# Accumulating stores for the second halves of the attention heads, and accumulating DMAs for seven of nine additions in the last products

## Chip, cores and metric

The kernel runs on one core of one Trainium2 chip. Its engines are TensorE (PE in the profile; its weight loads are PEld), VectorE (DVE), ScalarE (ACT), GpSimd (POOL) and SyncE (SP); SP, ACT and POOL issue DMAs, each from its own queue and in order. The metric is the time of one execution on the device, in microseconds (us); less is better.

## The reference

One decoder layer over 1024 tokens of width 1024, in float32:

```python
xn = rms_norm(x)
proj = xn @ w_in                # q,k,v of 8 heads x 64 | q,k,v,gate,forget code of 4 gated heads | merge gates
o_sb = stick_breaking_attention(q, k, v)       # causal, 8 heads, out[t] = sum_s w[t,s] v[s]
o_gla = gated_linear_attention(...)            # chunks, state S_t = diag(a_t) S_{t-1} + k_t^T v_t
y = sigmoid(gate_sb + b0) * (o_sb @ w_branch_sb) + sigmoid(gate_gla + b1) * (o_gla @ w_branch_gla)
h = x + y @ w_out
u, g = split(rms_norm(h) @ w_ffn_in)
h = h + (gelu(causal_conv(u)) * g) @ w_ffn_out
out = rms_norm(h)
```

## The kernel before

A scheduling layer takes the kernel's Python statements, tracks which tile or stretch of DRAM each instruction reads and writes, sets an order for every engine and adds the waits. Each engine runs its own instructions strictly in that order; a DMA is issued when its queue's turn comes and its waits are over. Tiles come from pools of equal buffers: `t2` (128x512 float32, 11 buffers), `t4` (128x1024, 14), `t8` (128x2048, 16), `bank` (PSUM, 8). A new tile waits until all readers of the buffer's last tile are done, DMAs included.

All float32 products are made of three rounded ones: an operand is split in a high part and a rest (`split`: a cast on ACT, L122, and a subtraction on VectorE, L113), and `mac` (L205) or its kin multiply high by high, high by rest, rest by high. The large products use seven products of halves instead of eight, which costs sums and differences of tiles.

The stages touched:

*Attention* (345 to about 536 us). `attend` walks over 4 pairs of heads and 4 blocks of 256 tokens. `weigh` makes one chunk of scores: products (L828), a sigmoid on ACT (L830) into a `t2` tile, a scan on VectorE (L833, L835). Up to six chunks later `turn_weights` transposes them on TensorE (L842), and `gather` multiplies them by the values (L871). As the values are split in a high part and a rest side by side, the product `po` holds two halves of 64 partitions that must be added: the head's output is the sum. ACT takes `po` to a `t2` tile `o` (L877), and SP stores the two halves in two places of the DRAM tile `osb_d` (L879). `heads(th)` later loads both places for 512 tokens (L855), adds them (L119) and splits the sum: `heads(0)` runs beside the last heads, `heads(1)` in the next stage. Products of the gates (L205) fill TensorE between all these.

On POOL's queue run the loads of keys and queries (L737, `fetched`), of the gated branch (`gv_d`, `qd_d`, `ki_d`: L950, L952, L953), the first weights of the first branch (L181), and `kt_d` (L962).

*States of the gated branch* (from 538 us): `states` multiplies `kt` by values (L970); VectorE takes the result to the state (L977, L979), POOL scales it (L981).

*Last products* (1168 to 1378 us): 1024 x 2816 times 2816 x 1024, as seven products of halves in four phases, each over 11 blocks of the inner dimension (`phase`, L1343): `first`, `second`, `third`, `fourth`. The rows of the residual `h` lie in `hr`, loaded in the first phase. After a phase `first_done` or `second_done` copies two results per 128 tokens from PSUM to `c` and `d` on ACT and puts additions into `later`, which the next phase takes out two per block from its third block on. There are five additions after the first phase and four after the second for each of four groups of 128 tokens. The last two phases add their own results straight from PSUM, normalise and store.

Of the kernel before, what the change touches and what calls it, by code (L numbers as in the profile page):

```python
# [12 lines left out]
AF = mybir.ActivationFunctionType  # L13
ALU = mybir.AluOpType
# [3 lines left out]
P = 128  # L18
# [4 lines left out]
HALF = 512  # L23
# [45 lines left out]
def block_kernel(ctx: ExitStack, tc: tile.TileContext, x, norm_mix_g, w_in, b_gate, w_alpha_up, b_alpha,  # L69
                 gla_norm_g, w_branch_sb, w_branch_gla, w_out, norm_ffn_g, w_ffn_in, conv_w, conv_b,  # L70
                 w_ffn_out, norm_final_g, out):
    nc = tc.nc
    x, out = x[0], out[0]
# [6 lines left out]
    def nm(s):  # L80
        uid[0] += 1
        return f"{s}_{uid[0]}"
# [7 lines left out]
    def t8(dt=F32R):  # L90
        return sb.tile([P, 2 * D], dt, tag="t8", name=nm("t8"), bufs=16)

    def t4(dt=F32):
        return sb.tile([P, D], dt, tag="t4", name=nm("t4"), bufs=T4)

    def t2(dt=F32):
        return sb.tile([P, HALF], dt, tag="t2", name=nm("t2"), bufs=T2)

    def bank():
        return ps.tile([P, HALF], F32, tag="bank", name=nm("bank"), bufs=8)  # L100

    def dram(name, rows, cols, dt=F32):
        return dp.tile([rows, cols], dt, tag=name, name=name)

    def by(a, k):
        return a.rearrange("p (k c) -> p k c", k=k)

    def quarter():

        return [by(t8(), 4) for _ in range(2)]  # L110

    def sub(o, a, b):
        nc.vector.tensor_tensor(out=o, in0=a, in1=b, op=ALU.subtract)  # L113
# [4 lines left out]
    def add(o, a, b):  # L118
        nc.vector.tensor_tensor(out=o, in0=a, in1=b, op=ALU.add)  # L119

    def split(h, l, src):
        nc.scalar.copy(h, src)  # L122
        sub(l, src, h.bitcast(F32))
# [45 lines left out]
    osb_d = dram("osb_d", 2 * SBH * SBD, S)  # L169
# [388 lines left out]
    for half in range(2):  # L558
# [5 lines left out]
        o = t2()  # L564
# [162 lines left out]
    HALVES = slice(0, 64), slice(64, 128)  # L727
# [117 lines left out]
    ob, first_heads = [], []  # L845

    def heads(th):

        ob.append(quarter())
        asked, added = deque(), deque()  # L850
        for k in range(6):
            if k < 4:
                asked.append((t2(), t2()))
                for n, v in enumerate(asked[-1]):
                    nc.sync.dma_start(v, osb_d[n * HALF + k * P:n * HALF + (k + 1) * P, th * HALF:(th + 1) * HALF])  # L855
            yield
            if k > 1:
                split(*(a[:, k - 2] for a in ob[th]), added.popleft())
            if k in range(1, 5):
                a, b = asked.popleft()  # L860
                add(a, a, b)
                added.append(a)
            yield

    def gather(head, tp, ah, al):
        po = bank()
        nb = 2 * tp + 2
        for b in range(nb):
            c0 = 0 if b < nb - 1 else P
            for n, a in enumerate((ah, al)):  # L870
                nc.tensor.matmul(po[:, c0:2 * P], vt[b][:, head, :], a[b // 4][:, b % 4, c0:],  # L871
                                 start=(b == 0 and n == 0), stop=(b == nb - 1 and n == 1))
        o = t2()[:, 0:2 * P]
        for n in range(2):
            c = slice(n * P, (n + 1) * P)
            i = head * NT + 2 * tp + n
            nc.scalar.activation(o[:, c], po[:, c], AF.Identity, bias=vend[:, i:i + 1])  # L877
        for n, r in enumerate(HALVES):
            nc.sync.dma_start(osb_d[n * HALF + head * 64:n * HALF + (head + 1) * 64, tp * 2 * P:(tp + 1) * 2 * P], o[r])  # L879
        if head == SBH - 1 and tp == 1:  # L880
            first_heads.append(heads(0))

    def attend():
# [47 lines left out]
        while todo:  # L931
            flush()
            while late:
                gather(*late.popleft())
            for v in first_heads:
                next(v, None)
            yield 2
# [220 lines left out]
    n = 0  # L1158
    for _ in gated():
        if n == HEADS_AT:  # L1160
            fill(heads(1), 12)
        n += 1
        fill(first_branch, n % GLA[1] < GLA[0])
        pace(0)
# [119 lines left out]
    acts, hr = [], []  # L1284
# [44 lines left out]
    def row(i, j):  # L1329
        return hr[i][:, j * HALF:(j + 1) * HALF]  # L1330

    later, ready = deque(), deque()
# [33 lines left out]
    def temps(i):  # L1366
        return spare8[:, i], spare[i // 2][:, i % 2 * HALF:(i % 2 + 1) * HALF]

    def first_done(i, p1, p7):
        c, d = temps(i)  # L1370
        nc.scalar.copy(c, p1)
        nc.scalar.copy(d, p7)
        later.append(lambda: add(row(i, 0), row(i, 0), c))
        later.append(lambda: add(row(i, 1), row(i, 1), c))
        later.append(lambda: add(d, d, c))
        later.append(lambda: add(row(4 + i, 0), row(4 + i, 0), d))
        later.append(lambda: add(row(4 + i, 1), row(4 + i, 1), d))

    def second_done(i, p5, p6):
        c, d = temps(i)  # L1380
        nc.scalar.copy(c, p5)
        nc.scalar.copy(d, p6)
        later.append(lambda: add(row(4 + i, 0), row(4 + i, 0), d))
        later.append(lambda: add(c, c, d))
        later.append(lambda: add(row(i, 1), row(i, 1), c))
        later.append(lambda: add(row(4 + i, 1), row(4 + i, 1), c))

    gfin = []

# [25 lines left out]
            mul(row(4 + i, 1), row(4 + i, 1), gfin[0][:, HALF:])  # L1415

    def fourth_done(i, p4):
        r = row(4 + i, 0)
        sub(r, r, p4)
        o = spare[i % 2]  # L1420
        a, b = ss[i]
        nc.scalar.activation(o[:, :HALF], r, AF.Square, accum_out=b)
        add(a, a, b)
        nc.scalar.activation(b, a, AF.Sqrt, bias=eps, scale=1.0 / D)
        nc.vector.reciprocal(a, b)
        nc.scalar.activation(o[:, HALF:], row(4 + i, 1), AF.Copy, scale=a)
        nc.vector.scalar_tensor_tensor(out=o[:, :HALF], in0=r, scalar=a, in1=gfin[0][:, :HALF],
                                       op0=ALU.mult, op1=ALU.mult)
        t = slice((4 + i) * P, (5 + i) * P)
        if i < 3:  # L1430
            nc.gpsimd.dma_start(out[t, :], o)
        else:
            nc.sync.dma_start(out[t, :HALF], o[:, :HALF])
            nc.scalar.dma_start(out[t, HALF:], o[:, HALF:])

    for n, _ in enumerate(jobs):
        if n == 0:
# [9 lines left out]
    spare = [t4() for _ in range(2)]  # L1447
    spare8 = by(t8(F32), 4)
    phase(first, 2, 0, first_done, residual)
    phase(second, 2, 0, second_done, last_norm)  # L1450
    phase(third, 2, TILED[0], third_done)
    phase(fourth, 1, TILED[1], fourth_done, squares)


# [25 lines left out]
```

## Time and profile before

| | us |
|---|---|
| median of 3 runs | 1386.52 (1386.4 to 1386.62) |
| the profiled execution | 1386.67 |
| its span, first to last instruction | 1384.8 |
| TensorE busy | 1372.4 |
| VectorE busy | 1064.6 |
| ACT busy | 643.9 |
| POOL busy | 136.3 |

Views of the trace give times from the start of the span. A line of the list of waits names the waiting engine, the tile and line it waited in, and what ended the wait; then the sum in us, how many times, and the longest. A group has the number of its instructions, then busy us and the mean ns of one, then the idle time of the engine just before them. A timeline row has start, length, engine, line, operation, what is written and read, how many instructions it merges (xN), and in brackets the idle time before it. A DMA row ends in the size and the time from issue to landing. A row of a stretch has its limits, its length, then busy us and instructions of PE, PEld, DVE, ACT and POOL, then the granted clock of TensorE, the DMA engines' busy share and GB/s.

### The profile page before, as it was taken

Reading aid. Unit: us, or ns where it says so; the run is one execution under the profiler, and the core shown is the slowest. Engines: PE = TensorE matmul, PEld = TensorE weight load, DVE = VectorE, ACT = ScalarE, POOL = GpSimd, SP = SyncE. Lnnn points to the kernel's source line nnn. Section 1 sums busy time; section 2 is a strip of 40 time slices with the busy share of each in tenths; the row PEclk is TensorE's granted clock in tenths of the full one; section 3 lists DMA queues with packets and bytes.
Section 4 is the critical chain, followed back from the end, with each engine's and each line's share of the span. In section 5 each row is a group of like instructions: output and inputs, shape, how many; then the busy total and the mean of one; then the engine's idle time right before and its main releaser. Section 6 shows DMA issues by size and latency. Waiting matters only on the chain.

```text
span 1384.8 us, 18329 instructions
## 1 busy us (share of the span) xinstructions
PE 1372.4 (99%) x6559; PEld 1138.8 (82%) x6559; DVE 1064.6 (77%) x1640; ACT 643.9 (46%) x1244; POOL 136.3 (10%) x233
## 2 busy tenths in 40 slices
PE   9999999999999999999999999999999999999997
PEld 6788888888888888888888788888888888888886
DVE  6388688874878877658348998998888977896765
ACT  7334445653766664724126443343333334454654
POOL 2002123101111002200000000000000000000000
PEclk9999999999999999999999999999999999999999
DMA  6335278448776567673325245554444537953332
GB/s 239 132 117 151 84 221 251 143 158 210 216 158 151 131 197 237 198 237 136 136 91 177 52 120 187 196 189 152 150 163 152 182 107 272 322 163 102 99 101 105
DMA packets 164108, 227.92 MB, mean 165 GB/s; under 512 B 10938, under 2 KB 105276, under 8 KB 163506
## 3 DMA queue, kind: packets, MB, share of 16 engines
q1 hardware_dynamic: 134944, 139.01, 33.0%
q0 software_dynamic: 22496, 73.73, 16.8%
q10 hardware_dynamic: 6578, 14.03, 2.7%
q8 instruction: 51, 0.84, 0.3%
q14 instruction: 39, 0.32, 0.1%
HBM read 160.28 MB, written 66.45 MB: 164 GB/s over the span
## 4 chain that ended last, share of the span: by engine, by line
PE 95%; DVE 3%; ACT 1%; issue 0%; DMA 0%; ACTq 0%; DVEq 0%
PE bank L205 58%; PE bank L1343 15%; PE bank L385 6%; PE bank L1210 6%; PE bank L871 3%; PE bank L828 2%; PE bank L842 2%; DVE t L113 2%; PE bank L494 1%; PE bank L340 1%; DVE t L119 1%; PE bank L562 1%; PE bank L1007 1%; PE bank L970 0%; PE bank L994 0%
## 5 line engine op out<-in xcount | busy, mean ns | idle before, releaser
L205 PE MATMUL bank<-t,t 128*128 128x512 f32 x3624 | 861.1, 393 | 0.9 <-DVE t L113 0.7
L205 PEld LDWEIGHTS bank<-t,t 128*128 128x128 f32 x3624 | 676.5, 188 | 143.1 <-DVE t L113 1.6
L113 DVE TENSOR_TENSOR t<-t,t 128x512 fp32r<-128x512 f32 (+3 forms) x655 | 434.6, 697 | 93.5 <-ACT t L122 87.2
L122 ACT CAST t<-t 128x512 fp32r<-128x512 f32 (+1 forms) x543 | 320.3, 627 | 325.4 <-DVE t L113 81.0
L119 DVE TENSOR_TENSOR t<-bank,t 128x512 f32<-128x512 f32 x266 | 179.3, 685 | 97.9 <-PE bank L205 54.9
L1343 PE MATMUL bank<-t,t 128*128 128x512 f32 x924 | 209.6, 389 | 0.0
L1343 PEld LDWEIGHTS bank<-t,t 128*128 128x128 f32 x924 | 173.5, 188 | 36.0
L113 DVE TENSOR_TENSOR t<-bank,t 128x512 fp32r<-128x512 f32 (+4 forms) x124 | 69.5, 574 | 27.5 <-ACT t L122 26.9
L1210 PE MATMUL bank<-t,t 128*128 128x512 f32 x384 | 88.8, 391 | 0.0
L1241 ACT ACTIVATE t<-t,vcol 128x1024 f32<-128x1024 f32 x22 | 27.4, 1245 | 127.5 <-DVE t L119 127.5
L113 DVE TENSOR_TENSOR t<-t 128x512 f32<-128x512 f32 x120 | 83.3, 701 | 4.1 <-DMA t<-in_w_ffn_in_dram 3.7
L1210 PEld LDWEIGHTS bank<-t,t 128*128 128x128 f32 x384 | 71.6, 188 | 14.6
L119 DVE TENSOR_TENSOR t<-t,t 128x512 f32<-128x512 f32 x115 | 75.5, 686 | 9.8 <-ACT t L628 8.6
L122 ACT CAST t<-bank 128x512 fp32r<-128x512 f32 (+3 forms) x120 | 60.3, 512 | 48.8 <-PE bank L842 26.8
L385 PE MATMUL bank<-t,t 128*128 128x512 f32 x336 | 77.9, 391 | 0.0
L385 PEld LDWEIGHTS bank<-t,t 128*128 128x128 f32 x336 | 62.7, 188 | 13.1 <-DVE t L113 0.2
L1243 DVE SCALAR_TENSOR_TENSOR t<-t,vcol,t 128x1023 f32<-128x1023 f32 (+1 forms) x44 | 56.3, 1279 | 14.1 <-ACT t L1241 13.9
L833 DVE TENSOR_TENSOR_SCAN t<-t,t 128x128 f32<-128x128 f32 (+1 forms) x64 | 51.6, 816 | 17.5 <-ACT t L830 17.2
L828 PE MATMUL bank<-t,t 128*128 128x128 f32 (+3 forms) x192 | 54.6, 369 | 0.0
L842 PE MATMUL bank<-ident,t 128*128 128x128 f32 x288 | 53.2, 273 | 0.0
L871 PE MATMUL bank<-t,t 128*128 128x256 f32 (+1 forms) x320 | 51.0, 276 | 1.2 <-ACT t L122 0.7
L830 ACT ACTIVATE t<-bank 128x128 f32<-128x128 f32 (+3 forms) x96 | 46.9, 507 | 7.2 <-DMA osb_d<-t 3.2
(164 smaller groups left out, 813.5 us busy)
## 6 DMA issues: line engine op xcount, KB each, us to landing
t<-in_w_ffn_in_dram SPq DMA_DIRECT2D x50, 512.0 KB, 5.1
t<-in_w_in_dram SPq DMA_DIRECT2D x43, 512.0 KB, 5.3
act_d<-t POOLq DMA_DIRECT2D x22, 512.0 KB, 5.8
t<-in_w_ffn_out_dram SPq DMA_DIRECT2D x22, 512.0 KB, 7.6
wsum_d<-t POOLq DMA_DIRECT2D x22, 512.0 KB, 4.5
t<-act_d SPq DMA_DIRECT2D x22, 512.0 KB, 5.9
t<-wsum_d SPq DMA_DIRECT2D x44, 256.0 KB, 3.1
t<-in_w_ffn_out_dram SPq DMA_DIRECT2D x33, 256.0 KB, 2.7
```

The source lines that it names most:

```text
L113: nc.vector.tensor_tensor(out=o, in0=a, in1=b, op=ALU.subtract)
L119: nc.vector.tensor_tensor(out=o, in0=a, in1=b, op=ALU.add)
L122: nc.scalar.copy(h, src)
L205: nc.tensor.matmul(pt, a[:, kk], b[:, kk], start=start and kk == 0 and m == 0, stop=stop and kk == k - 1 and m == 2)
L385: nc.tensor.matmul(pt, a[:, k % 4, t], b, start=k == 0 and m == 0, stop=k == NK - 1 and m == 2)
L828: nc.tensor.matmul(z[:, 0:w], q[:, a, e, ts_], kk[:, e, b0 * P:b1 * P], start=a == 0, stop=a == 1)
L833: nc.vector.tensor_tensor_scan(out=kr, data0=kr, data1=above[:, 0:w], initial=1.0, op0=ALU.mult, op1=ALU.max)
L842: nc.tensor.transpose(pt[:, b * P:(b + 1) * P], ke[:, b * P:(b + 1) * P], ident)
L871: nc.tensor.matmul(po[:, c0:2 * P], vt[b][:, head, :], a[b // 4][:, b % 4, c0:], start=(b == 0 and n == 0), stop=(b == nb - 1 and n == 1))
L1210: nc.tensor.matmul(pt, a[:, k % 4, t], b, start=(k == 0 and m == 0), stop=(k == NK - 1 and m == 2))
L1243: nc.vector.scalar_tensor_tensor(out=cv[:, i:], in0=av[:, :S - i], scalar=col(V_CW, (2 - i) * NF + f), in1=cv[:, i:], op0=ALU.mult, op1=AL ...
L1343: nc.tensor.matmul(pts[m][i], a[:, t], b, start=(k == 0 and x_ == 0), stop=(k == NH - 1 and x_ == 2))
```

## The change

In `gather` the first half is stored to `osb_d` by SP as before, at the place of the sum, and the second half is stored by POOL to the same place with an addition done by the DMA. `heads` then loads one tile where it loaded two, and adds nothing. In the last products seven of the nine additions per 128 tokens become DMAs from POOL that add `c` or `d` to the rows in `hr`; the two that make a new `d` or `c` stay on VectorE. The last phase writes its output over `hr` instead of into `spare`.

```diff
     def heads(th):
-        asked, added = deque(), deque()
+        asked = deque()
         for k in range(6):
             if k < 4:
-                asked.append((t2(), t2()))
-                for n, v in enumerate(asked[-1]):
-                    nc.sync.dma_start(v, osb_d[n * HALF + k * P:n * HALF + (k + 1) * P, th * HALF:(th + 1) * HALF])
+                asked.append(t2())
+                nc.sync.dma_start(asked[-1], osb_d[k * P:(k + 1) * P, th * HALF:(th + 1) * HALF])
             yield
             if k > 1:
-                split(*(a[:, k - 2] for a in ob[th]), added.popleft())
-            if k in range(1, 5):
-                a, b = asked.popleft()
-                add(a, a, b)
-                added.append(a)
+                split(*(a[:, k - 2] for a in ob[th]), asked.popleft())
             yield
...
     def gather(head, tp, ah, al):
-        for n, r in enumerate(HALVES):
-            nc.sync.dma_start(osb_d[n * HALF + head * 64:n * HALF + (head + 1) * 64, tp * 2 * P:(tp + 1) * 2 * P], o[r])
+        dst = osb_d[head * 64:(head + 1) * 64, tp * 2 * P:(tp + 1) * 2 * P]
+        nc.sync.dma_start(dst, o[HALVES[0]])
+        nc.gpsimd.dma_start(dst, o[HALVES[1]], accum_op=ALU.add)
...
+    def onto(o, a):
+        nc.gpsimd.dma_start(o, a, accum_op=ALU.add)
+
     def first_done(i, p1, p7):
         c, d = temps(i)
         nc.scalar.copy(c, p1)
         nc.scalar.copy(d, p7)
-        later.append(lambda: add(row(i, 0), row(i, 0), c))
-        later.append(lambda: add(row(i, 1), row(i, 1), c))
+        onto(row(i, 0), c)
+        onto(row(i, 1), c)
         later.append(lambda: add(d, d, c))
-        later.append(lambda: add(row(4 + i, 0), row(4 + i, 0), d))
-        later.append(lambda: add(row(4 + i, 1), row(4 + i, 1), d))
+        later.append(lambda: onto(row(4 + i, 0), d))
+        later.append(lambda: onto(row(4 + i, 1), d))

     def second_done(i, p5, p6):
-        later.append(lambda: add(row(4 + i, 0), row(4 + i, 0), d))
+        onto(row(4 + i, 0), d)
         later.append(lambda: add(c, c, d))
-        later.append(lambda: add(row(i, 1), row(i, 1), c))
-        later.append(lambda: add(row(4 + i, 1), row(4 + i, 1), c))
+        later.append(lambda: onto(row(i, 1), c))
+        later.append(lambda: onto(row(4 + i, 1), c))
...
     def fourth_done(i, p4):
-        o = spare[i % 2]
-        nc.scalar.activation(o[:, :HALF], r, AF.Square, accum_out=b)
+        nc.scalar.activation(spare8[:, i], r, AF.Square, accum_out=b)
-        nc.scalar.activation(o[:, HALF:], row(4 + i, 1), AF.Copy, scale=a)
-        nc.vector.scalar_tensor_tensor(out=o[:, :HALF], in0=r, scalar=a, in1=gfin[0][:, :HALF], op0=..., op1=...)
+        nc.scalar.activation(q, q, AF.Copy, scale=a)
+        nc.vector.scalar_tensor_tensor(out=r, in0=r, scalar=a, in1=gfin[0][:, :HALF], op0=..., op1=...)
```

The lines behind `heads` move up by four or five: L877 becomes L872, L950 to L962 become L946 to L958, L970 becomes L966, L1343 becomes L1339. POOL's accumulating stores of the heads are L875, SP's plain ones L874, the last products' accumulations L1367.

The order in which the instructions stand on POOL, at the end of attention. `t4_1027` and `t4_1030` are first weights of the first branch, `t4_1035` and `t4_1037` the two halves of `kt`. Before:

```order
L953 DMA t8_964_4970<-ki_d_84 128x1024
L181 DMA t4_1027_5307<-in_w_branch_sb_dram 128x4x256
L181 DMA t4_1030_5315<-in_w_branch_sb_dram 128x4x256
L962 DMA t4_1035_5325<-kt_d_85 128x1024
L962 DMA t4_1037_5328<-kt_d_85 128x1024
L981 TENSOR_SCALAR t4_1036_5327<-t2_1033_5323,emid0_992 128x128
```

And now, with the outputs of the last five gathers (`t2_969` to `t2_1022`) between them; `kt` is now `t4_1031` and `t4_1033`:

```order
L875 DMA osb_d_88<-t2_969_4993 64x256
L875 DMA osb_d_88<-t2_992_5089 64x256
L181 DMA t4_1023_5295<-in_w_branch_sb_dram 128x4x256
L875 DMA osb_d_88<-t2_1014_5206 64x256
L875 DMA osb_d_88<-t2_1016_5228 64x256
L181 DMA t4_1026_5303<-in_w_branch_sb_dram 128x4x256
L875 DMA osb_d_88<-t2_1022_5282 64x256
L958 DMA t4_1031_5313<-kt_d_85 128x1024
L958 DMA t4_1033_5316<-kt_d_85 128x1024
L977 TENSOR_SCALAR t4_1032_5315<-t2_1029_5311,emid0_992 128x128
```

The two `kt` loads and the second weight load stand behind the accumulating stores of the last three gathers.

TensorE's order at the same place, with the semaphores that each row waits for, now:

```order
L205 MATMUL bank_1018_5242<-t8_59_336,t4_1003_5139 128x512
L966 MATMUL bank_1040_5338<-t8_963_4966,t4_1031_5313 128x256 [waits DMASW6_49,DMASW0_49]
L205 MATMUL bank_1043_5346<-t8_974_5015,t4_1024_5297 128x512 [waits PE_49,Activation_49]
L205 MATMUL bank_1043_5346<-t8_975_5016,t4_1024_5297 128x512
L205 MATMUL bank_1043_5346<-t8_974_5015,t4_1024_5297 128x512 [waits DVE_49]
L205 MATMUL bank_1043_5346<-t8_974_5015,t4_1024_5297 128x512
L205 MATMUL bank_1043_5346<-t8_975_5016,t4_1024_5297 128x512
L205 MATMUL bank_1043_5346<-t8_974_5015,t4_1024_5297 128x512
L966 MATMUL bank_1044_5353<-t8_963_4966,t4_1033_5316 128x256 [waits DMASW1_49,PE_49]
```

Before, the same nine stood there in the same order (as L205 and L970, with `t4_1035` and `t4_1037`): TensorE's order is kept, and the first reader of `kt` still stands thirteen matmuls of L205 behind the last gather.

The third place is ACT's order near the second head's output, with the waits. `t2_573` is the tile that a chunk's sigmoid (L830) writes. Before:

```order
L720 DMA gate_d_86<-t2_564_3213 128x512 [waits Activation_49]
L877 ACTIVATE t2_566_3225<-bank_565_3216,t2_478_2890 128x128
L830 ACTIVATE t2_570_3244<-bank_569_3241 128x256 [waits DMAHW7_49,DMAHW6_49]
L830 ACTIVATE t2_573_3255<-bank_572_3252 128x512 [waits DVE_49,PE_49]
L122 CAST t4_528_3081<-bank_582_3281 128x4x128 [waits PE_49]
```

And now:

```order
L720 DMA gate_d_86<-t2_564_3213 128x512 [waits Activation_49]
L872 ACTIVATE t2_566_3225<-bank_565_3216,t2_478_2890 128x128
L830 ACTIVATE t2_570_3244<-bank_569_3241 128x256 [waits DVE_49]
L830 ACTIVATE t2_573_3255<-bank_572_3252 128x512 [waits DMAHW5_49,DMASW5_49,PE_49]
L122 CAST t4_528_3081<-bank_582_3281 128x4x128 [waits PE_49]
```

The order is the same, but `t2_573` has got the buffer of the second head's output `t2_550`, and waits for its plain store (a DMA of SP's queue, HW) and its accumulating one (of POOL's, SW).

More of the change, by code (lines that the diff above doesn't have):

```diff
@@ L1417, in fourth_done @@
     def fourth_done(i, p4):
-        r = row(4 + i, 0)
+        r, q = row(4 + i, 0), row(4 + i, 1)
         sub(r, r, p4)
-        o = spare[i % 2]
         a, b = ss[i]
-        nc.scalar.activation(o[:, :HALF], r, AF.Square, accum_out=b)
+        nc.scalar.activation(spare8[:, i], r, AF.Square, accum_out=b)
         add(a, a, b)
@@ L1425, in fourth_done @@
         nc.vector.reciprocal(a, b)
-        nc.scalar.activation(o[:, HALF:], row(4 + i, 1), AF.Copy, scale=a)
-        nc.vector.scalar_tensor_tensor(out=o[:, :HALF], in0=r, scalar=a, in1=gfin[0][:, :HALF],
-                                       op0=ALU.mult, op1=ALU.mult)
+        nc.scalar.activation(q, q, AF.Copy, scale=a)
+        nc.vector.scalar_tensor_tensor(out=r, in0=r, scalar=a, in1=gfin[0][:, :HALF], op0=ALU.mult, op1=ALU.mult)
         t = slice((4 + i) * P, (5 + i) * P)
         if i < 3:
-            nc.gpsimd.dma_start(out[t, :], o)
+            nc.gpsimd.dma_start(out[t, :], hr[4 + i])
         else:
-            nc.sync.dma_start(out[t, :HALF], o[:, :HALF])
-            nc.scalar.dma_start(out[t, HALF:], o[:, HALF:])
+            nc.sync.dma_start(out[t, :HALF], r)
+            nc.scalar.dma_start(out[t, HALF:], q)
     for n, _ in enumerate(jobs):
```

## The prediction

> **What bounds the kernel now.** I read the page first: its span, the busy line, the granted clock and the chain that ended last.
>
> ```profile
> span 1384.8 us, 18329 instructions
> ...
> PE 1372.4 (99%) x6559; PEld 1138.8 (82%) x6559; DVE 1064.6 (77%) x1640; ACT 643.9 (46%) x1244; POOL 136.3 (10%) x233
> ...
> PEclk9999999999999999999999999999999999999999
> ...
> PE 95%; DVE 3%; ACT 1%; issue 0%; DMA 0%; ACTq 0%; DVEq 0%
> ```
>
> TensorE is busy for 1372.4 of 1384.8 us and makes up 95% of the chain. The second view is the list of TensorE's own waits, which says what there is to win:
>
> ```profile
> PE bank L464 <- DVE t L457: 1.6, 1, 1.6
> PE bank L435 <- POOL ident masks.py:199: 1.5, 1, 1.5
> PE bank L205 <- DVE t L113: 0.7, 1, 0.7
> PE bank L871 <- ACT t L122: 0.7, 1, 0.7
> PE bank L871 <- DVE t L113: 0.5, 1, 0.5
> ```
>
> TensorE waits 5.0 us in all. Two of the waits (L871, 0.7 and 0.5 us) lie where the diff works; the last-product phases (L1343) are not in the list. So work taken from VectorE is worth almost nothing, and a new wait on TensorE is paid in full, because its stream has no slack to give back. The question is what the change puts in front of TensorE.
>
> **Part 1: seven of nine additions in the last products.** VectorE loses 28 of 36 additions. Their price is in the groups of the second and third phases, and the matmuls' row of the page tells whether anybody waited:
>
> ```profile
> L119 DVE TENSOR_TENSOR t<-t,t 128x512 f32<-128x512 f32 x36 | 23.1, 684 | 0.3 <-ACT t L1382 0.3
> ```
>
> ```profile
> L1343 PE MATMUL bank<-t,t 128*128 128x512 f32 x924 | 209.6, 389 | 0.0
> ```
>
> They are the 36; 28 x 0.684 = 19 us of VectorE go, and TensorE idles 0.0 us before these 924 matmuls, so the gain is 0. What comes in its place is 28 accumulating DMAs of 256 KB on POOL's queue. The stretches in which they fall:
>
> ```profile
> 1228.00:1288.00 60.00, 60.00 (x266) 49.69 (x266) 45.75 (x75) 29.15 (x54) 0.00 (x0) 1.00 0.36 109
> 1288.00:1348.00 60.00, 60.00 (x267) 49.69 (x266) 42.71 (x69) 31.43 (x60) 1.07 (x2) 1.00 0.31 94
> ```
>
> POOL (0.00 and 1.07 us busy) and the DMA engines (share 0.36 and 0.31) are nearly free. 28 x 256 KB is 7.3 MB; even counted three times (read both, write one) it is 22 MB over 120 us, 183 GB/s beside the 109 and 94 moved now. The sums are read a phase later, up to 60 us after they start. Cover: the next phase's matmuls. I take 0; the bad end is a rival below. The last tile's output in place, instead of through `spare`, keeps the same instructions: 0.
>
> **Part 2: the heads' halves.** 32 of the 64 stores of `osb_d` (L879) move from SP to POOL and add to what SP's store has written; 8 of 16 reloads (L855) and 8 additions go. The additions go from ACT's and VectorE's path near the end of attention: ACT's splits there wait for them (ACT's waits between 520 and 545):
>
> ```profile
> ACT t L122 <- DVE t L119: 8.5, 2, 4.3
> ```
>
> ACT in order behind these splits feeds the 0.7 us of `L871 <- ACT t L122`. I take -0.7, with 0 and -1.2 (both L871 waits) as ends.
>
> Each accumulating store has to wait until its partner has landed, and POOL issues in order, so everything behind it on POOL stands. The order in the change's section shows what is behind the last three: one weight load of the first branch and both `kt_d` loads, which the state products (L970) read. Before, POOL's timeline there is:
>
> ```profile
> 526.20 0.77 POOL L181 DMA_DIRECT2D t<-in_w_branch_sb_dram  x1 [35.08 <-issue]
> 527.70 0.76 POOL L181 DMA_DIRECT2D t<-in_w_branch_sb_dram  x1 [0.72 <-PE bank L205]
> 528.82 1.17 POOL L962 DMA_DIRECT2D t<-kt_d  x2 [0.36 <-PE bank L871]
> ```
>
> And TensorE's, with the last head's gather at 533.44 and the first two users of `kt` at 538.20 and 540.02:
>
> ```profile
> 533.44 1.89 PE L871 MATMUL bank<-t,t 128*128 128x256 f32 x15
> 535.16 3.19 PE L205 MATMUL bank<-t,t 128*128 128x512 f32 x13
> 538.20 0.59 PE L970 MATMUL bank<-t,t 128*128 128x256 f32 x2
> 538.44 1.75 PE L205 MATMUL bank<-t,t 128*128 128x512 f32 x6
> 540.02 1.03 PE L970 MATMUL bank<-t,t 128*128 128x256 f32 x4
> ```
>
> The last gather leaves ACT, and SP stores it, here:
>
> ```profile
> 535.37 0.63 ACT L877 ACTIVATE t<-bank,t 128x128 f32<-128x128 f32 x2 [2.32 <-PE bank L871]
> ...
> 538.98 0.61 ACT L122 CAST t<-t 128x512 fp32r<-128x512 f32 x1
> ```
>
> ```profile
> 536.02 1.08 SPq L879 DMA_DIRECT2D osb_d<-t  x2
> ```
>
> The DMA view, asked for the moment of one issue, gives one landing: that store, the two `kt` loads, and the first branch's weights, a load of the same size on the same queue when it was emptier:
>
> ```profile
> osb_d<-t SPq DMA_DIRECT2D x1, 64.0 KB, 1.9
> ```
>
> ```profile
> t<-kt_d POOLq DMA_DIRECT2D x1, 512.0 KB, 5.5
> ```
>
> ```profile
> t<-kt_d POOLq DMA_DIRECT2D x1, 512.0 KB, 7.1
> ```
>
> ```profile
> t<-in_w_branch_sb_dram POOLq DMA_DIRECT2D x1, 512.0 KB, 3.9
> ```
>
> Now step by step. Store issued 536.0, landed 537.9. POOL issues the accumulating store, 0.6 us (half of 1.17 for two), and starts the first `kt` load at 538.5 instead of 528.8. It lands 5.5 later, at 544.0, and TensorE wants it at 538.2: 5.8 us of standing still, since the row behind L970 in TensorE's order can't pass it. The second load starts at 539.1 and lands 7.1 later, at 546.2; TensorE wants it 1.8 after the first: 545.8, another 0.4. Together 6.2 us. Ends: with 3.9 for both loads 542.4 - 538.2 = 4.2; with 7.1 for the first and 8.7 (the same 1.6 more) for the second, 7.4 + 0.4 = 7.8. I take 6.2, because SP's reloads of `osb_d` start in the same microseconds as they did around the loads of before. The second weight load has until 538.98, when ACT splits it: with 3.9 to land it may leave POOL as late as 535.1, 7.4 us later than before (527.70), so 0. The earlier shift of all this work doesn't help: the whole chain starts from TensorE's own gather.
>
> **The tiles held longer.** An output tile is freed when the accumulating store has landed, not the plain one. The tightest reuse I found is the second head's output: the next writer of its buffer is now a weigh sigmoid (L830), ACT's order shows its new wait. Rows: the store, issued behind the two loads of `x21_d`, the sigmoid pair, its scan, and TensorE's transposes of it:
>
> ```profile
> 363.06 1.09 SPq L879 DMA_DIRECT2D osb_d<-t  x2
> ```
>
> ```profile
> osb_d<-t SPq DMA_DIRECT2D x1, 64.0 KB, 7.4
> ```
>
> ```profile
> 371.29 0.86 ACT L830 ACTIVATE t<-bank 128x256 f32<-128x256 f32 x2
> ```
>
> ```profile
> 372.50 1.28 DVE L835 TENSOR_TENSOR_SCAN t<-t,t,zero 128x512 f32<-128x512 f32 x1
> ```
>
> ```profile
> 374.94 0.60 PE L842 MATMUL bank<-ident,t 128*128 128x128 f32 x4
> ```
>
> ```profile
> DMA to landing us min/median/max: 1.9/4.4/8.4
> ```
>
> The last row is of all 64 plain stores of L879. No row shows an accumulating store. It can't be quicker than a plain one of its size (1.9), since it reads its target too; the slowest, 8.4, is the other end; I take the median, 4.4. Store landed 370.5, accumulation landed 374.9, against the second sigmoid at 371.7 (half of the pair's time behind 371.29): ACT stands 3.2 us. TensorE has 374.94 - 373.78 = 1.2 us of slack behind the scan, so 2.0 reach it. Ends: 0 (with 1.9 ACT stands 0.7, inside the slack) and 6.0 (with 8.4).
>
> **The clock.** The granted clock in windows at the start and at the end:
>
> ```profile
> 4.90:8.30 3.40, 1.81 (x9) 0.83 (x9) 2.00 (x4) 2.55 (x6) 0.00 (x0) 1.00 1.04 404
> 8.30:11.70 3.40, 3.40 (x10) 2.00 (x9) 3.23 (x5) 3.37 (x8) 2.50 (x2) 0.50 1.05 401
> ...
> 1377.60:1380.40 2.80, 0.00 (x0) 0.00 (x0) 1.60 (x4) 1.61 (x4) 0.53 (x1) 1.00 0.47 187
> 1380.50:1384.80 4.30, 0.00 (x0) 0.00 (x0) 0.06 (x1) 0.03 (x1) 0.00 (x0) 0.50 0.33 122
> ```
>
> After 3.4 us with TensorE half idle the next 3.4 ran at 0.50, and at the end 0.50 was granted within 2.9 us of its last matmul. A stall of 6 us should bring one such stretch: at half speed 3.4 us lose 1.7. Part of it falls in the stall itself: I take 1.3, with 0 and 1.7 as ends. The Trainium skill (TensorE: Matmul & The Clock Gate, "What's actually happening") says that an idle window of about 3.4 us halves the clock until a busy one has passed; the two rows agree with it, and by the page alone the term would be 1.7, without the rule 0.
>
> **The sum.** +6.2 (kt) +2.0 (tile) +1.3 (clock) -0.7 (heads' additions) + 0 (last products) = +8.8. The profiled execution took 1386.67 us (span 1384.8 and 1.9 around it): 1395.5. It is 0.15 above the median of the runs, 1386.52, so the forecast is 1395.3. Ends: 4.2 + 0 + 0 - 1.2 = +3.0 gives 1389.5; 7.8 + 6.0 + 1.7 - 0 = +15.5 gives 1402.0.
>
> **Rivals.** *POOL isn't held* (not slower): if the accumulating stores were queued with their wait and POOL went on, the `kt` loads would start only three issues of 0.6 later, at 530.6 and 531.2, and land 5.5 and 7.1 behind that, at 536.1 and 538.3, before TensorE wants them at 538.2 and 540.0. The time would be 1386.5 - 0.7 = 1385.8. The point that decides: the first `kt` load has to leave POOL by 532.7 (538.2 - 5.5). Against it stands how POOL's loads of keys and queries behave now:
>
> ```profile
> L737 POOL DMA_DIRECT2D t<-sqkh_d x24 | 14.0, 588 | 116.6 <-PE bank L828 83.5 <-DVE t L113 29.3 <-PE bank L205 3.5
> ```
>
> POOL itself sat idle for 83.5 of 116.6 us until TensorE had let their buffers go. The Trainium skill (DMA: Bandwidth & Descriptors, "Anatomy of one DMA") says that the DMA engines don't wait on semaphores and the issuing sequencer does; by that rule this rival falls, and the row agrees. Chance 0.07.
>
> *Accumulating stores are slow* (8.4 us or more each): then the tile of the second head costs 6.0, and the same place recurs in later head pairs; counted twice more at half that, 6.0 more. 1395.3 + 4.0 + 6.0 = 1405.3. Nothing shows it, nothing excludes it. Chance 0.07.
>
> *The last products wait*: if the 256 KB accumulations went one after another at 8.4 us, the first phase's 16 would take 134 us where 60 are free, and the second phase's copies would stand 74 us: 1460. The free DMA share speaks against it. Chance 0.03.
>
> *A real gain* of over 2.8 us would have to come out of 1.9 us of TensorE's waits behind the start and the last tile's 7 us, which the change doesn't shorten. Chance 0.03.
>
> **How the numbers follow.** The forecast's case has 0.80 and lies wholly above 1389.3 (0.2%, 2.8 us, is about what a measurement of this kernel can tell from no change). The range is its bounds, 1389.5 to 1402.0, reached up to 1405.3 to take in the slow stores: it leaves out 0.13. Slower by over 0.2%: 0.80 + 0.07 + 0.03 = 0.90; within it 0.07; faster 0.03.
>
> **What would show it.** TensorE's waits should gain a line `L966 <- DMA t<-kt_d` of about 6 us near 540; POOL's timeline should show both `kt` issues behind the last accumulating store of L875; the granted clock should drop to 0.50 once behind that stall; ACT's L830 should wait some 3 us for `osb_d<-t` near 372; the four last phases should still run without TensorE idle. The prediction is wrong if `kt` leaves POOL before 533, or if a line of the last products (L1339) shows up among TensorE's waits.

## The result and the profile after

The changed kernel takes 1396.79 us (median of 4 runs, 1395.26 to 1396.95), the kernel before beside it 1386.56 us (1386.4 to 1386.62). The ratio is 1.0071, with a 95% interval of 1.0054 to 1.0089: slower, as forecast, and 1.5 us from the 1395.3 forecast. The profiled execution took 1396.89 us. Its page, the rows that answer to those shown of before:

```profile
span 1395.2 us, 18356 instructions
...
PE 1376.5 (99%) x6559; PEld 1140.7 (82%) x6559; DVE 1043.3 (75%) x1604; ACT 643.3 (46%) x1244; POOL 186.5 (13%) x293
...
PE 85%; DVE 6%; DMA 4%; issue 4%; ACT 1%; POOL 1%; SPq 0%; DVEq 0%; ACTq 0%; POOLq 0%
```

VectorE lost 21 us of work, and the span grew by 10.4. TensorE's share of the chain that ended last falls from 95% to 85%, and DMA, which had none, has 4%. TensorE's list of waits says where:

```profile
PE bank L966 <- DMA t<-kt_d: 7.7, 1, 7.7
...
PE bank L205 <- DVE t L113: 0.8, 1, 0.8
...
PE bank L1339 <- DVE t L113: 0.3, 1, 0.3
...
PE bank L842 <- DVE t L113: 0.3, 1, 0.3
```

One wait is new and large, for `kt`. The two waits at the gathers (L871, 0.7 and 0.5 us) have no counterpart of their size; two of 0.3 are new. POOL's timeline at the end of attention:

```profile
532.48 1.69 POOL L875 DMA_DIRECT2D osb_d<-t  x2 [6.73 <-ACT t L122]
533.74 1.26 POOL L181 DMA_DIRECT2D t<-in_w_branch_sb_dram  x1
538.93 0.83 POOL L875 DMA_DIRECT2D osb_d<-t  x1 [3.94 <-DMA osb_d<-t]
539.49 1.41 POOL L958 DMA_DIRECT2D t<-kt_d  x2
548.07 0.37 POOL L977 TENSOR_SCALAR t<-t,emid 128x128 f32<-128x128 f32 x1 [7.18 <-DVE t L973]
```

POOL stood for 3.94 us, released by `DMA osb_d<-t`: the landing of SP's plain store, the partner of the last accumulating one. Only then came the two loads of `kt`, at 539.5 and 540.1, where they had stood at 528.8 and 529.4. The landing of SP's store, asked for the moment of its issue, and that of the first `kt` load:

```profile
osb_d<-t SPq DMA_DIRECT2D x1, 64.0 KB, 2.4
```

```profile
t<-kt_d POOLq DMA_DIRECT2D x1, 512.0 KB, 6.5
```

TensorE resumes the moment it lands (539.49 + 6.5 = 546.0):

```profile
533.41 1.88 PE L866 MATMUL bank<-t,t 128*128 128x256 f32 x15
535.13 3.19 PE L205 MATMUL bank<-t,t 128*128 128x512 f32 x13
546.01 1.22 PE L966 MATMUL bank<-t,t 128*128 128x256 f32 x2 [7.68 <-DMA t<-kt_d]
546.67 3.12 PE L205 MATMUL bank<-t,t 128*128 128x512 f32 x6
```

The gather that starts it all ran at the same time as before (533.41 against 533.44): nothing earlier in the program had been lost by then. The last row shows a second loss. Six matmuls of L205 take 3.12 us where the same six took 1.75. The granted clock (the column ahead of the DMA share) in stretches of 3.4 us:

```profile
536.44:539.84 3.40, 1.88 (x9) 1.22 (x7) 0.26 (x1) 1.48 (x3) 0.91 (x2) 1.00 0.88 263
539.84:543.24 3.40, 0.00 (x0) 0.00 (x0) 1.04 (x2) 1.47 (x3) 1.05 (x2) 1.00 0.91 303
543.24:546.64 3.40, 0.63 (x2) 0.55 (x3) 0.00 (x0) 0.62 (x1) 0.00 (x0) 0.50 0.99 359
546.64:550.04 3.40, 3.40 (x10) 2.64 (x9) 0.58 (x2) 0.62 (x1) 0.37 (x1) 0.50 0.74 221
550.04:553.44 3.40, 3.40 (x17) 2.84 (x16) 1.96 (x6) 0.00 (x0) 0.74 (x2) 1.00 0.67 230
```

One stretch without a matmul, then two at half the clock: 10 matmuls in the fourth row, 17 in the fifth. The clock comes back 4.0 us after the matmuls did, which costs 2.0.

For the account, the start of each matmul was taken from both traces (6559 in each, nearly in the same order) and subtracted. The columns are the time in the kernel before at which the matmul starts, then the end of the last matmul and of the program; the rows are the delay in us, each set to 0 at 26.7 us, since the first 27 us differ by -0.4 to +0.35 from one execution to the next. The last column is the time from the end of the last matmul to the end of the program.

```
               377.0  460.5  532.8  538.2  544.7  555.1 1305.1 1311.9 |  last    end | tail
before          0      0      0      0      0      0      0      0    |  0      0    | 7.23
after           0.81   0.81  -0.37   7.48   9.47   9.46   9.37  10.38 | 10.38  10.04 | 6.89
e1_heads        1.82   1.82   0.23   7.89  10.36  10.36  10.36  10.36 | 10.36  12.62 | 9.49
e2_last        -0.02  -0.02  -0.02  -0.02  -0.02  -0.03  -0.03   0.79 |  0.79   1.42 | 7.86
e3_kt_ahead     0.82   0.82  -0.39  -0.40  -0.40   1.45   1.42   2.16 |  2.16   1.83 | 6.91
e4_pool_plain   0.00   0.00   0.01   5.09   7.83   7.83   7.82   7.82 |  7.82   9.98 | 9.39
e5_one_behind   0.37   0.37  -1.30   0.23   0.35   2.43   2.45   3.54 |  3.54   3.21 | 6.90
e6_plain_over   0.09   0.09  -1.59   5.67   7.70   7.69   7.67   8.45 |  8.45   8.12 | 6.90
e7_squares      0.26   0.25  -1.41  -1.41  -1.41   1.35   1.33   1.96 |  1.96   1.62 | 6.89
e8_copies       0.00   0.78  -1.00  -1.00  -1.00   0.23   0.24   0.91 |  0.91   0.44 | 6.76
e9_squares     -0.00   1.13  -0.53  -0.53  -0.53   0.43   0.40   0.40 |  0.40  -0.08 | 6.76
e10_heads      -0.01   1.01  -0.68  -0.68  -0.68  -0.66  -0.76  -0.76 | -0.76   1.19 | 9.18
```

The row of the changed kernel is the whole story: +0.8 near 375 us, 0.5 more by 500 us, both given back and 0.4 gained by 533; then +7.85 at `kt`, +2.0 by the clock, nothing for 760 us, +1.0 where the fourth phase begins. The tail is 0.3 shorter.

### The profile page after: what moved, and what is told of

Same layout as the page of the kernel before. It is cut to its first block, busy times and chain, and to the rows that moved or that the text cites. A ratio compares the mean times of both kernels' runs of the same rounds, so it can differ in the third digit from the quotient of the medians.

```text
span 1395.2 us, 18356 instructions
## 1 busy us (share of the span) xinstructions
PE 1376.5 (99%) x6559; PEld 1140.7 (82%) x6559; DVE 1043.3 (75%) x1604; ACT 643.3 (46%) x1244; POOL 186.5 (13%) x293
## 4 chain that ended last, share of the span: by engine, by line
PE 85%; DVE 6%; DMA 4%; issue 4%; ACT 1%; POOL 1%; SPq 0%; DVEq 0%; ACTq 0%; POOLq 0%
PE bank L205 57%; PE bank L1339 7%; PE bank L385 5%; PE bank L1206 5%; DVE t L113 3%; PE bank L866 2%; PE bank L828 2%; DMA t<-t 2%; PE bank L842 2%; DVE t L119 1%; DMA osb_d<-t 1%; PE bank L340 1%; POOL t L1367 1%; PE bank L562 1%; PE bank L1003 1%
## 5 line engine op out<-in xcount | busy, mean ns | idle before, releaser
L205 PE MATMUL bank<-t,t 128*128 128x512 f32 x3624 | 863.0, 394 | 0.9 <-DVE t L113 0.8
L205 PEld LDWEIGHTS bank<-t,t 128*128 128x128 f32 x3624 | 677.7, 188 | 143.3 <-DVE t L113 1.6
L1339 PE MATMUL bank<-t,t 128*128 128x512 f32 x924 | 210.2, 390 | 0.4 <-DVE t L113 0.3
L1339 PEld LDWEIGHTS bank<-t,t 128*128 128x128 f32 x924 | 173.5, 188 | 37.0 <-DVE t L113 0.6
L119 DVE TENSOR_TENSOR t<-t,t 128x512 f32<-128x512 f32 x79 | 52.3, 688 | 9.4 <-ACT t L628 8.6
L1243 POOL DMA_DIRECT2D act_d<-t x22 | 11.7, 531 | 352.3 <-DVE t L116 352.3
L830 ACT ACTIVATE t<-bank 128x128 f32<-128x128 f32 (+3 forms) x96 | 47.4, 511 | 10.7 <-DMA gate_d<-t 4.5
```

Of the source, the lines that this page charges most:

```text
L205: nc.tensor.matmul(pt, a[:, kk], b[:, kk], start=start and kk == 0 and m == 0, stop=stop and kk == k - 1 and m == 2)
L830: nc.scalar.activation(ke[:, 0:w], z[:, 0:w], AF.Sigmoid, scale=-SBD ** -0.5)
L1339: nc.tensor.matmul(pts[m][i], a[:, t], b, start=(k == 0 and x_ == 0), stop=(k == NH - 1 and x_ == 2))
```

## The experiments

Theory: the `kt` loads were put behind accumulating stores that hold POOL's queue; stall and clock are the price. Rivals: the accumulating DMAs themselves are the cost, by their length or by the load on the DMA engines, in the heads or in the last products. The table above holds the delays of all ten runs.

### Each part alone

e1_heads_alone takes the heads' part of the change (the hunks of `heads` and `gather` in the diff above) and leaves the last products as they were; e2_last_alone takes the other hunks alone.

> The heads' accumulating stores alone; the last products are those of the kernel before. Theory (the kt loads stand behind the last accumulating stores on POOL's queue): TensorE's wait for kt of 7 to 8 us and one half-clock stretch of 1.7 to 2.0 us are all here, so +9.5 to +10, about 1396.3. Rival (the accumulating DMAs of the last products cost TensorE several us by filling the DMA engines): this part alone gives +7 or less, under 1393.5.

> The last products' 28 accumulating DMAs and the output in place alone; the heads are those of the kernel before. Theory: +0.8 us at the start of the fourth phase (as in the changed kernel's trace, 1309 us into it) and 0.3 less behind the last matmul: 1386.8 to 1387.3, no line of kt among TensorE's waits. Rival (the DMA engines, filled for 34 and 22 us, delay weight loads): +3 us or more, over 1389.5.

The heads alone: 1398.73 us (ratio 1.0088, 1.0074 to 1.0101). The last products alone: 1388.52 us (1.0013, 1.0004 to 1.0022). Of each, a row of TensorE's waits:

```profile
PE bank L966 <- DMA t<-kt_d: 7.5, 1, 7.5
```

```profile
PE bank L1343 <- DVE t L113: 0.3, 1, 0.3
```

All of the stall and the clock's loss (7.66 and 2.47 by the table) are in the heads; the second part alone loses 0.8 at the fourth phase and nothing at `kt`. The times are 2.4 and 1.2 us above what was expected, though. Most of that is the tail, the time behind the last matmul (below, what was not expected): 2.3 us longer in e1, and 0.6 longer in e2 where 0.3 less was expected.

### The order alone

e3_kt_ahead is the changed kernel with three stores moved behind `kt` on POOL:

```diff
-        nc.gpsimd.dma_start(dst, o[HALVES[1]], accum_op=ALU.add)
+        def rest():
+            return nc.gpsimd.dma_start(dst, o[HALVES[1]], accum_op=ALU.add)
+
+        if tp == NT // 2 - 1 or tp == 2 and head == SBH - 1 if head >= SBH - 2 else False:
+            owing.append(rest)
+        else:
+            rest()
...
-            nc.gpsimd.dma_start(kt, kt_d[p * P:(p + 1) * P, :])
+            last_kt[:] = [nc.gpsimd.dma_start(kt, kt_d[p * P:(p + 1) * P, :])]
...
     fetch_rest()
+    for store in owing:
+        after(store(), last_kt[0])
```

> The changed kernel with one order changed: the last three accumulating stores of the heads stand behind the kt loads on POOL, not ahead of them. Theory: kt leaves POOL at 529 and 530 and lands by 536.5, before TensorE wants it at 538.2; the wait of 7.7 us and the half-clock stretch go together, and 1386.7 to 1387.4 is left. Rival (the accumulating stores and SP's reloads of osb_d load the DMA engines and make kt late wherever it stands): a wait for kt of 3 us or more stays, over 1390.

The condition picks the last three gathers. 1388.16 us (1.0011, 1.0002 to 1.002), 0.8 above what was expected. POOL's rows and TensorE's longest wait:

```profile
529.68 1.09 POOL L964 DMA_DIRECT2D t<-kt_d  x2 [0.58 <-PE bank L866]
536.02 1.84 POOL L876 DMA_DIRECT2D osb_d<-t  x2 [5.25 <-ACT t L872]
```

```profile
PE bank L1009 <- POOL t L1001: 1.6, 1, 1.6
```

The wait for `kt` is gone, and the half-clock stretches with it: -0.40 at 538.2 and at 544.7. No accumulating DMA was taken out for that, only three of them moved behind `kt`: the order makes the stall. The wait in the row above is one that the stall had covered: SP's last reload of `osb_d` waits for the last accumulating store to land, two branch weights stand behind it on SP, ACT has their splits ahead of two copies of the gated branch, POOL masks those copies, and TensorE waits for the mask. In the kernel before those weights left SP later still (547.3 against 545.6), but ACT took the copies ahead of the splits. I had not seen it.

### The place without the addition, and a smaller dose

e4_pool_plain is the kernel before with one queue changed; e5_one_behind keeps only the very last accumulating store behind `kt`, with the edit of e3_kt_ahead for one gather.

```diff
-            nc.sync.dma_start(osb_d[n * HALF + head * 64:...], o[r])
+            (nc.sync, nc.gpsimd)[n].dma_start(osb_d[n * HALF + head * 64:...], o[r])
```

> The kernel before, with the heads' second halves stored plainly by POOL, each to its own place: no accumulation and no wait for the partner's landing, only the place in POOL's queue. Theory (a store in order behind its gather holds what is behind it, accumulating or not): the last store waits for ACT until 536.0, kt leaves POOL at 536.6 instead of 539.5, lands 5.5 to 6.5 later at 542.1 to 543.1, TensorE waits 3.9 to 4.9 and loses 1.3 to 2.0 to the clock: 1391.5 to 1393.5. Rival (only the accumulation's wait for its partner makes the stall): no change, 1386 to 1387.

> The changed kernel with only the very last accumulating store put behind the kt loads on POOL; the two before it stay ahead. A smaller dose of the same wait. Theory: POOL waits for the store partner that lands at 532.6 in the changed kernel, kt leaves at 534.4 and 535.0 and lands 5.5 to 7 later, TensorE waits 1.7 to 2.7 us. The clock falls in stretches of 3.4 us after a mostly idle one: so 0 if the stall splits over two stretches, 2.0 if not. With 0.8 at the fourth phase 1389 to 1393. Rival (what counts is that an accumulating store is under way at all): 7 us of waiting as before, 1396.

e4_pool_plain: 1395.80 us (1.0066, 1.0054 to 1.0079). e5_one_behind: 1389.80 us (1.0024, 1.0015 to 1.0033). Their waits, first e4, then e5:

```profile
PE bank L970 <- DMA t<-kt_d: 4.9, 1, 4.9
```

```profile
PE bank L972 <- DMA t<-kt_d: 1.4, 1, 1.4
```

Nothing is added and no partner awaited in e4, and TensorE still stands 4.9 us. A plain store waits for the gather's output as well, and in e4 that output came late itself. ACT's rows, then POOL's:

```profile
535.48 1.14 ACT L122 CAST t<-t 128x512 fp32r<-128x512 f32 x2 [3.72 <-DMA t<-in_w_branch_sb_dram]
536.52 0.62 ACT L877 ACTIVATE t<-bank,t 128x128 f32<-128x128 f32 x2
```

```profile
537.43 0.55 POOL L879 DMA_DIRECT2D osb_d<-t  x1 [4.66 <-ACT t L877]
537.98 1.11 POOL L962 DMA_DIRECT2D t<-kt_d  x2
```

In e4 the first weights of the branch, too, left POOL behind stores, at 531.2 and 532.0 instead of 526.2 and 527.7. ACT waited 3.72 us for them and took the last gather at 536.5; in the kernel before it was 535.4. That is the same effect of a place in the queue, by a second path that the changed kernel doesn't have.

The place alone thus makes a stall of 4.9 us, but the other 2.8 of the 7.7 are not all the partner's landing. Counted from the start of the last gather, `kt` left POOL after 4.8 us in e4 and after 6.1 in the changed kernel, and took 5.0 and 6.5 us to land: 1.3 us are the later issue and 1.5 a slower load, for which no run here shows the cause. The expected time was missed by 2.3 us: the tail is 2.2 us longer, and the clock cost 2.7 instead of 1.3 to 2.0. The clock in stretches of 3.4 us, in e4 and then in e5:

```profile
538.40:541.80 3.40, 0.00 (x0) 0.00 (x0) 1.29 (x2) 1.46 (x3) 0.69 (x2) 1.00 0.90 266
541.80:545.20 3.40, 2.17 (x5) 1.80 (x6) 0.58 (x2) 0.00 (x0) 0.12 (x1) 0.50 0.98 357
545.20:548.60 3.40, 3.40 (x9) 2.66 (x9) 0.62 (x3) 0.00 (x0) 0.37 (x2) 0.50 1.05 401
548.60:552.00 3.40, 3.40 (x16) 2.80 (x16) 2.04 (x5) 0.03 (x1) 1.31 (x3) 1.00 0.27 94
```

```profile
537.80:541.20 3.40, 2.65 (x13) 2.16 (x13) 1.86 (x5) 1.13 (x3) 0.19 (x1) 1.00 0.92 300
541.20:544.60 3.40, 3.40 (x17) 2.80 (x16) 2.37 (x7) 1.74 (x3) 2.17 (x5) 1.00 0.79 274
```

In e4 the clock was back 5.6 us after the matmuls, and the shorter stall lost more by it (2.74) than the longer one of the changed kernel (2.0). A stall of 1.4 us cost no clock at all. The half-clock time is a whole number of such stretches: two in the changed kernel and in e4, and three (540.8 to 551.0) in e1. The Trainium skill (TensorE: Matmul & The Clock Gate, "What's actually happening") has the window of about 3.4 us running freely, so that what one meets depends on where in the window the work falls; these half-clock times of 6.8, 6.8 and 10.2 us agree.

### The addition left out

e6_plain_over stores the second halves over the first ones, by POOL at the same places of the order and with the same wait; the sum of the halves is left out.

```diff
-        nc.gpsimd.dma_start(dst, o[HALVES[1]], accum_op=ALU.add)
+        nc.gpsimd.dma_start(dst, o[HALVES[1]])
```

> The changed kernel, but the second halves are stored over the first ones instead of added to them (plain DMAs from POOL at the same places of the order, with the same wait for the partner): the addition itself is left out. Theory (the order on POOL's queue and the wait, not the adding): TensorE's wait for kt is 7 to 8 us and the time that of the changed kernel, 1396 to 1397.5. Rival (the adding makes the DMAs slow and with them kt): the wait falls to 6.5 or less and the time to 1395 or less.

1395.30 us (1.006, 1.0047 to 1.0072). The wait for `kt` in this kernel, then the time to landing of these 32 stores, in the changed kernel and in this one:

```profile
PE bank L966 <- DMA t<-kt_d: 7.1, 1, 7.1
```

```profile
DMA to landing us min/median/max: 2.5/2.7/5.2
```

```profile
DMA to landing us min/median/max: 1.9/2.1/4.8
```

The theory has the wait right and the time 0.7 us too high; the rival has neither. The wait stays at 7.1, so the adding doesn't make it. The median store lands 0.6 us sooner without the addition. That this makes the kernel faster isn't shown: the time is 1.5 us lower, but the two intervals overlap, and 1.2 of it stand at 533 us, ahead of `kt` (-1.59 against -0.37), where e5 and e7, which do add, have -1.30 and -1.41.

### Can the rest be repaired?

e7_squares_first is e3_kt_ahead with the order of four accumulations changed. e8_copies_first keeps the first two heads as they were before and puts the two copies ahead of the late splits on ACT. e9_squares_apart gives the squares of the last phase a result tile of their own. The three edits, each on top of the one before:

```diff
-        later.append(lambda: onto(row(i, 1), c))
         later.append(lambda: onto(row(4 + i, 1), c))
+        owed_rows.append(lambda: onto(row(i, 1), c))
+        if i == 3:
+            later.extend(owed_rows)
```

```diff
     def gather(head, tp, ah, al):
+        if head < 2:
+            nc.sync.dma_start(osb_d[HALF + head * 64:HALF + (head + 1) * 64, ...], o[HALVES[1]])
+            nc.sync.dma_start(osb_d[head * 64:(head + 1) * 64, ...], o[HALVES[0]])
+            return
...
     def split(h, l, src):
-        nc.scalar.copy(h, src)
+        c = nc.scalar.copy(h, src)
+        if len(copies) == 2:
+            after(c, copies[1])
```

```diff
-            nc.scalar.activation(spare8[:, i], row(4 + i, 1), AF.Square, accum_out=ss[i][0])
+            nc.scalar.activation(t2(), row(4 + i, 1), AF.Square, accum_out=ss[i][0])
```

> The kernel with kt ahead of the last three stores, and in the second phase's sums the four accumulations that the squares of the last phase read (second half of rows 4 to 7) ahead of the four that only the third phase's end reads. Theory (the accumulations run one after another at 1.3 to 2.0 us and the squares on ACT wait for the last one, so that the fourth phase's first splits are late): the 0.3 us wait at the fourth phase and the 0.5 behind it go, 1387.0 to 1387.8. Rival (the weight loads are late because the DMA engines are full): the wait at the fourth phase stays, 1388.2.

> All repairs together: kt ahead of the last three stores, the squares' sums first, the first two heads stored and added as in the kernel before (24 accumulating stores are left of 32), and on ACT the two copies of the gated branch ahead of the splits of the late branch weights. Theory: the waits at 374 us (0.5), 461 us (0.5, if it comes from the same tiles), 553 us (1.6) and in the fourth phase (0.8) go, the two waits at L871 (1.2) of the kernel before stay away: 1385.0 to 1386.2. Rival (what one wait gives back the next takes): 1387 or more.

> All repairs, and the squares of the last phase write their unused result to a tile of their own instead of over the tile that the last accumulations still read (the squares' sums first had left the wait of 0.3 us at the fourth phase, because their output tile is the source of the last four accumulations). Theory (the wait is for the reading DMAs, not for the sums): ACT's squares follow the second, sixth, seventh and eighth accumulation of the second phase, the wait at the fourth phase goes and the 0.5 us lost there with it: 1385.8 to 1386.5. Rival (the weights come late): the wait at the fourth phase stays, 1386.7.

e7: 1387.93 us (1.0011, 1.0002 to 1.002). e8: 1386.69 (1.0003, 0.9994 to 1.0011). e9: 1386.61 (0.9996, 0.9987 to 1.0005). None of them met what its theory said: e7 is 0.1 us above it, e8 0.5, e9 0.1. The order of the sums did not help; the wait at the fourth phase stayed, in e7 and in e8, and ACT's longest wait there grew (TensorE's row in e7, then ACT's in the changed kernel and in e7):

```profile
PE bank L1347 <- DVE t L113: 0.3, 1, 0.3
```

```profile
ACT t L1414 <- issue: 5.2, 1, 5.2
```

```profile
ACT t L1424 <- issue: 10.1, 2, 9.9
```

My reason for e7 was wrong. The squares write their unused result over `c`, the tile that the last accumulations still read, so they wait for all of them whatever stands first. An addition on VectorE had let `c` go within 0.7 us. With a tile of its own (e9) the delay at 1311.9 is that at 1305.1, 0.40, and TensorE's wait is gone. ACT still waits there for the sums that the squares read, in four pieces:

```profile
ACT t L1435 <- DMA t<-t: 9.3, 4, 4.1
```

Between 544.7 and 555.1 us e8 loses 1.2 where e7 lost 2.8. With the first two heads as before the delay at 377 us is gone, but 0.8 to 1.1 come at 460.5 (e8 to e10), which e8 was expected to remove; their cause was not looked for. All repairs together reach the kernel before and don't measurably beat it: TensorE is busy for 99% either way.

e10_heads_repaired has the heads of e8 and the last products of the kernel before:

```diff
-        onto(row(i, 0), c)
-        onto(row(i, 1), c)
+        later.append(lambda: add(row(i, 0), row(i, 0), c))
+        later.append(lambda: add(row(i, 1), row(i, 1), c))
...
```

> The repaired heads alone: 24 accumulating stores, kt ahead of the last three, the two copies ahead of the late splits; the last products are those of the kernel before. POOL issues 205 DMAs. Theory: the last matmul ends 0.3 to 1 us earlier than in the kernel before (the two waits at L871, 1.2, are gone, little comes back), and POOL's last drain, 6.35 us with 181 DMAs, 6.97 with 209 and 8.1 to 8.3 with 213, is 6.4 to 7.0 with 205 and takes 0.1 to 0.6 of it: 1386.0 to 1386.8. Rival (the drain goes by the kind of the DMAs, not by their number): 8 us or more or under 4, 1388 or 1385.8.

1388.99 us (1.0016, 1.0007 to 1.0025), although its last matmul ends 0.76 us earlier than that of the kernel before, as expected. The tail took it: 9.18 us instead of 7.23. Neither idea about its cause held.

## Why the prediction was right, point by point

- *TensorE pays every new wait in full, and VectorE's work is worth nothing.* So it was: 21 us of VectorE went, and no gain shows at the places they went from but the heads'.
- *`kt`, forecast +6.2, bounds 4.2 to 7.8.* The mechanism is shown: with the order changed it goes (e3), with the place alone most of it comes (e4), with a smaller dose 1.4 us come (e5). The size was low: 7.7 us of wait, 7.85 of delay. The plain store took 2.4 us to land, not 1.9; POOL needed another 0.5 between the landing and the issue; `kt` took 6.5, not 5.5. The 0.4 of the second load didn't come: TensorE at half clock needed it later. The reason given for 5.5, that SP's reloads of `osb_d` start in the same microseconds as before, was misread: before, none started from 523 to 537.8 us, and that first load was under way from 528.8 to 534.3. Whether the reloads made the 6.5 is open, as in e4 `kt` landed in 5.0 beside them.
- *The clock, forecast +1.3, bounds 0 to 1.7.* Measured 2.0, outside the bounds, and 2.5 and 2.7 in e1 and e4. The step that failed is "one such stretch", part of it in the stall: two followed, as the first of them was itself mostly idle, and it ends where the grid of stretches says. How idle a stretch must be these rows don't settle: 1.81 us of matmuls in 3.4 lost the clock at the start of the kernel before, 1.88 kept it here (at 536.44).
- *Tiles held longer, forecast +2.0, bounds 0 to 6.0.* The place was right. ACT's rows of the second head's reuse, and the accumulating store that it waited for:

```profile
371.60 0.38 ACT L830 ACTIVATE t<-bank 128x256 f32<-128x256 f32 x1
373.16 0.60 ACT L830 ACTIVATE t<-bank 128x512 f32<-128x512 f32 x1 [1.19 <-PE bank L866]
```

```profile
osb_d<-t POOLq DMA_DIRECT2D x1, 64.0 KB, 4.1
```

  The row names TensorE as the releaser, but the store, issued at 368.95, landed at 373.1, and the sigmoid began 0.1 later. ACT stood 1.2 us, not 3.2, since the plain store landed after 5.0 us instead of 7.4; 0.8 reached TensorE. I had found one such place; 0.5 came at others. The 0.8 is one execution's: with the same order here e7 lost 0.26, e5 0.37 and e1 1.82.
- *Heads' additions, forecast -0.7, end -1.2.* From 500 to 533 us the delay falls by 1.7 (1.31 at 500 us to -0.37): more than the end of the bounds, and it paid for what the tiles had cost. It falls at the two places where L871 had waited, by 0.7 near 525 and by 1.0 near 532. The row of 8.5 us that stood for ACT's path was half misread: one of its two waits ended at 544.4, behind the last gather, and could not feed it. Net, the heads were 0.4 ahead when `kt` stopped them.
- *Last products, forecast 0.* Measured +1.0, and this step was the one argued worst. "Nearly free" DMA engines were not free:

```profile
1234.00:1268.00 34.00, 34.00 (x152) 28.17 (x151) 23.70 (x37) 17.35 (x33) 13.85 (x16) 1.00 1.04 242
1296.00:1318.00 22.00, 22.00 (x99) 18.23 (x98) 10.17 (x16) 8.74 (x19) 10.48 (x12) 1.00 1.01 202
```

  Sixteen accumulations fill the DMA engines for 34 us and twelve for 22, about 2 us each; their share is 1.0 where it was 0.3. "Read a phase later" was wrong for the sums that the squares read, as ACT's 9.3 us in e9 show, but TensorE didn't pay for these. It paid for the source tiles (in e8 the delay still grows by 0.67 where the fourth phase begins, in e9, where the squares leave these tiles alone, by nothing), and the prediction named no one who waited for them. It said that a line of L1339 among TensorE's waits would prove it wrong; on this term it does.
- *The tail* had no term: 0.3 less here, up to 2.3 more in the experiments.

The sum came out 1.5 us below the measurement because two terms that were too small (`kt` and clock, 2.35 together) and a missing one (1.0) stand against two that were too high (tiles, less the heads' gain, 1.7). The way and the main cause were foreseen; that the number came so near is in part luck. The rival that POOL isn't held is refuted by the 3.94 us of its timeline; the one of slow accumulating stores by their longest landing, 5.2 us.

## What to carry to other kernels

When work moves to a queue that issues in order, read what stands behind it there and who reads that first: the moved DMA waits for its own input, and loads that had been early become late by the whole of that wait. A stall of TensorE costs more than its length if it leaves a stretch of the clock idle; one of 1.4 us cost nothing more, those of 4.9 to 7.7 us another 2.0 to 2.7. An addition by DMA takes load off an engine that may have had time to spare, and holds its source and target longer: ask not only when the sum is read, but who writes the source next.

## What the runs showed of the hardware that was not expected

At the end of the program POOL executes a drain, which the profile's views don't count as busy. It starts with POOL's last store and ends the program where it is longer than about 6 us. Its length differs by kernel, with nothing in the kernel at that place to explain it:

```
                     POOL's DMAs   drain us   last matmul to end us
before                   181         6.35        7.23
e10_heads_repaired       205         7.65        9.18
e2_last_alone            209         6.97        7.86
e4_pool_plain            213         8.14        9.39
e1_heads_alone           213         8.30        9.49
e8, e9                   233         3.44        6.76
after, e3, e5, e6, e7    241         3.65        6.89 to 6.91
```

It explains why e1, e4 and e10 end 1.9 to 2.3 us later than their matmuls say. It doesn't go by the number of DMAs alone (205 against 209), nor by their kind (e1 accumulates, e4 doesn't). All kernels with 233 DMAs or more have the short drain, e6 with plain stores of the heads among them; why is open.

The second surprise is the scatter: kernels with accumulating stores and `kt` in time ran from 1386.4 to 1391.4 us (e7) and 1384.8 to 1388.3 (e9) in 11 runs each, the kernel before from 1386.1 to 1388.1 in 21. The delays at 377 and 460 us differ between executions of the same order as well (0.82 and 0.26 in e3 and e7). Which landings make it was not tried.
